# A softmax with relative-position bias: loads and stores on two queues, rows in one long run per partition

## The chip, the cores and the metric

The kernel runs on one core of a Trainium2 chip. The metric is the device time of one execution in microseconds; the time before is the median of three runs, 1329.67 us (1329.32 to 1330.35). One more execution was taken with the hardware profiler. Times inside it are counted from its first instruction.

The engines that matter here are VectorE (DVE in the profile), ScalarE (ACT), GpSimd (POOL), SyncE (SP), which issues transfers, and the 16 DMA engines, which move data between the memory (HBM) and the on-chip buffer. Each of SyncE and ScalarE has a queue of its own into the DMA engines; a transfer is cut into packets, one contiguous run of bytes each.

## What is computed

```python
B, H, S, max_rel = 2, 8, 2112, 16
rel = pos[:, None] - pos[None, :]                       # row minus column
bias = rel_bias[:, np.clip(rel, -16, 16) + 16]          # (H, S, S) from (H, 33)
x = logits + bias[None]                                 # logits: (B, H, S, S) float32
x = x - x.max(axis=-1, keepdims=True)
out = exp(x) / exp(x).sum(axis=-1, keepdims=True)
```

There are 2 x 8 x 2112 = 33,792 rows of 2112 floats, 8448 bytes each, so 285.5 MB are read and as much is written. The bias of a row is a constant on the far left, a constant on the far right and a ramp of 33 values around the diagonal. Seen from one row to the next it only slides by one column, so a single strip that is longer than a row holds the bias of all neighbouring rows as windows of it.

## The kernel before

**Tiling.** A partition owns blocks of W = 33 consecutive rows. 64 partitions hold one head and the other 64 the next head, so one pass of the outer loop (k, of K = 4) covers two heads of both batches. Within a pass, a block is cut into chunks of 6, 5, 6, 5, 6 and 5 rows for each batch, NT = 12 chunks, 48 in all. A chunk is one buffer of four (`X0` to `X3`): 128 partitions with 5 or 6 rows each, loaded by one transfer and stored by one transfer, one packet of 41 or 50 KB for each partition.

**The strip.** At the start of each pass `strip(k)` builds, on DVE, the strip `F` of the two heads (lines 143 to 158). The table `rel_bias` comes in once, by a small transfer on ScalarE's queue (line 107).

**One chunk.** `add(m)` waits for the chunk's load and then runs, for each row, one DVE instruction (line 173) that adds the strip's window, negates and keeps the row's extreme. `exps(m)` runs the exponential of each row on ACT (line 181), each as soon as its add is done, and sums it. `scale(m)` waits on DVE for all exponentials of the chunk, takes the reciprocals (line 189) and scales the first DV = 3 rows (line 193); `scale_rest(m)` scales the other 2 or 3 on ACT (line 198). Only then does DVE start the next chunk's adds.

**Queues.** All large transfers are issued by SyncE in one order that is written out by hand, `turn`: store chunk n, wait until the store of chunk n - 1 has landed, load chunk n + 3 into the buffer that it has freed. Before a store, SyncE waits for the scaled rows (semaphores `scaled` and `scaledA`). Loads and stores thus stand in one queue, one behind the other. The last chunk is stored in two parts, 3 and 2 rows. DVE, ACT and SyncE run loops (`Fori`) over the passes; inside a pass everything is written out.

Of the kernel before, what the change touches and what calls it, by code (L numbers as in the profile page):

```python
# [15 lines left out]
def kernel(  # L16
# [6 lines left out]
    nc = tc.nc  # L23
# [2 lines left out]
    assert S == S2  # L26
    MR = 16
    W = 2 * MR + 1
    NB = S // W
    K = H // 2  # L30
    assert NB * W == S and 2 * NB == P and H % 2 == 0
    FW = S + W - 1
    BIG = 3.0e38
    NBUF = 4
    SIZES = [6, 5, 6, 5, 6, 5]
    R = max(SIZES)
    assert sum(SIZES) == W

    CH = [(b, sum(SIZES[:i]), r) for b in range(B) for i, r in enumerate(SIZES)]
    NT = len(CH)  # L40
    assert NT % NBUF == 0
# [3 lines left out]
    F = io.tile([P, FW], FP32, tag="F", name="F")  # L45
    rbP = io.tile([P, H // 2, W], FP32, tag="rbP", name="rbP")
    rbK = io.tile([P, W], FP32, tag="rbK", name="rbK")
    rest = io.tile([P, NB], FP32, tag="rest", name="rest")
    nmax = io.tile([P, NBUF * R], FP32, tag="nmax", name="nmax")
    tot = io.tile([P, NBUF * R], FP32, tag="tot", name="tot")  # L50
    rec = io.tile([P, NBUF * R], FP32, tag="rec", name="rec")
    ps = ctx.enter_context(tc.tile_pool(name="ps", bufs=1, space=bass.MemoryType.PSUM))
    Z = ps.tile([P, 512], FP32, tag="Z", name="Z")
    eq, lt, gt = (Z[:, i * NB : (i + 1) * NB] for i in range(3))
# [12 lines left out]

    with tc.tile_critical(no_gpsimd_drain=True):  # L68
# [13 lines left out]
        def take(eng, sem, n):  # L82
            eng.wait_ge(sem, n).then_inc(sem, -n)  # L83


        def load(k, m):
            b, r = m % NBUF, CH[m][2]
            nc.sync.dma_start(out=X[b][:, 0 : r * S], in_=rows(logits, k, m, 0, r)).then_inc(ld[b], 16)

        def store(k, m, s0=0, n=None):  # L90
            b, n = m % NBUF, n or CH[m][2]
            if s0 < DV:
                take(nc.sync, scaled, DV)
            if s0 + n > DV:
                take(nc.sync, scaledA, s0 + n - DV)
            nc.sync.dma_start(
                out=rows(out, k, m, s0, n), in_=X[b][:, s0 * S : (s0 + n) * S]
            ).then_inc(st[b], 16)

        for m in range(NBUF):  # L100
            load(0, m)

        Q = 32
        step = list(F.ap[0])[0]
        nc.vector.memset(F[:, 0 : H * W], 0.0).then_inc(zero, 1)  # L105
        nc.scalar.wait_ge(zero, 1)
        nc.scalar.dma_start(
            out=bass.AP(tensor=F.tensor, offset=F.offset, ap=[[Q * step, P // Q], [1, H * W]]),
            in_=bass.AP(tensor=rel_bias.tensor, offset=rel_bias.offset, ap=[[0, P // Q], [1, H * W]]),
        ).then_inc(rb, 16)  # L110
        for p0 in (0, NB):
            nc.gpsimd.iota(  # L112
                F[p0 : p0 + NB, H * W : H * W + NB], pattern=[[-1, NB]], base=0,
                channel_multiplier=1, allow_small_or_imprecise_dtypes=True,
            ).then_inc(idx, 1)

        v = nc.vector
        done = [0]
# [11 lines left out]
        iq = F[:, H * W : H * W + NB]  # L130
        for m, op in ((eq, ALU.is_equal), (lt, ALU.is_gt), (gt, ALU.is_lt)):
            then(v.tensor_scalar(out=m, in0=iq, scalar1=0.0, scalar2=None, op0=op))  # L132
        v.wait_ge(rb, 16)
        then(v.stream_shuffle(out=F[:, 0 : H * W], in_=F[:, 0 : H * W], mask=[0] * Q))  # L134
        settle()
        for h in range(2):
            p = slice(h * NB, (h + 1) * NB)
            src = bass.AP(tensor=F.tensor, offset=F[p].offset + h * W,
                          ap=[[list(F.ap[0])[0], NB], [2 * W, K], [1, W]])
            then(v.tensor_copy(out=rbP[p], in_=src))  # L140
        settle()

        def strip(k):

            then(v.tensor_copy(out=rbK[:, :], in_=rbP[:, bass.ds(k, 1), :]))  # L145
            settle()
            low, high = rbK[:, W - 1 : W], rbK[:, 0:1]
            blocks = view(F, MR, [[W, NB], [1, W]])
            then(v.tensor_tensor(out=blocks, in0=view(eq, 0, [[1, NB], [0, W]]),  # L149
                                 in1=view(rbK, W - 1, [[0, NB], [-1, W]]), op=ALU.mult))  # L150
            then(v.tensor_scalar(out=rest, in0=lt, scalar1=low, scalar2=None, op0=ALU.mult))  # L151
            then(v.tensor_copy(out=F[:, 0:MR], in_=low.to_broadcast([P, MR])))  # L152
            then(v.tensor_copy(out=F[:, FW - MR : FW], in_=high.to_broadcast([P, MR])))  # L153
            settle()
            then(v.scalar_tensor_tensor(out=rest, in0=gt, scalar=high, in1=rest, op0=ALU.mult, op1=ALU.add))  # L155
            settle()
            then(v.tensor_tensor(out=blocks, in0=blocks, in1=view(rest, 0, [[1, NB], [0, W]]), op=ALU.add))  # L157
            settle()

        def row(m, i):  # L160
            return X[m % NBUF][:, i * S : (i + 1) * S]
# [2 lines left out]
            c = m % NBUF * R + i  # L164
            return t[:, c : c + n]

        DV = 3

        def add(m):
            take(v, ld[m % NBUF], 16)  # L170
            j, r = CH[m][1:]
            for i in range(r):
                v.tensor_tensor_reduce(  # L173
                    out=row(m, i), in0=row(m, i), in1=F[:, W - 1 - j - i : W - 1 - j - i + S],
                    scale=-1.0, scalar=BIG, op0=ALU.add, op1=ALU.min, accum_out=col(nmax, m, i),
                ).then_inc(added, 1)

        def exps(m):
            for i in range(CH[m][2]):
                take(nc.scalar, added, 1)  # L180
                nc.scalar.activation(  # L181
                    out=row(m, i), in_=row(m, i), func=ACTF.Exp, scale=-1.0, bias=col(nmax, m, i),
                    accum_out=col(tot, m, i),
                ).then_inc(expd, 1)

        def scale(m):
            r = CH[m][2]
            take(v, expd, r)
            v.reciprocal(out=col(rec, m, 0, r), in_=col(tot, m, 0, r)).then_inc(inv, 1)  # L189
            v.wait_ge(inv, 1).then_inc(inv, -1)  # L190
            v.sem_inc(invA, 1)
            for i in range(DV):
                v.tensor_scalar_mul(out=row(m, i), in0=row(m, i), scalar1=col(rec, m, i)).then_inc(scaled, 1)  # L193

        def scale_rest(m):
            take(nc.scalar, invA, 1)
            for i in range(DV, CH[m][2]):
                nc.scalar.activation(  # L198
                    out=row(m, i), in_=row(m, i), func=ACTF.Copy, scale=col(rec, m, i),
                ).then_inc(scaledA, 1)  # L200
# [19 lines left out]
        store(0, 0)  # L220
        with nc.Fori(0, K - 1, 1, engines=[ENG.SP]) as k:
            turn(k, 1, NT + 1)
        turn(K - 1, 1, NT - 3)
        for m in range(NT - 3, NT - 1):
            store(K - 1, m)
        r = CH[NT - 1][2]
        store(K - 1, NT - 1, 0, DV)
        store(K - 1, NT - 1, DV, r - DV)
        for b in range(NBUF):
            take(nc.sync, st[b], 32 if b == (NT - 1) % NBUF else 16)  # L230


# [28 lines left out]
```

## Time and profile before

| | before |
|---|---|
| median of the runs | 1329.67 us |
| the profiled execution's own time | 1329.3 us |
| its span, first to last instruction | 1327.5 us |
| DVE busy | 819.7 us, 62% |
| ACT busy | 808.8 us, 61% |
| SyncE's DMA queue: packets' time as a share of 16 engines | 99.8% |
| moved | 571.00 MB, mean 430 GB/s |

In the lines of the profile an instruction stands with its line in the kernel, its engine, its operation and its operands (`out<-in`, partitions x elements). In the windows each line has the stretch in microseconds, its length, the busy time of DVE, ACT and POOL with the number of instructions, a clock (of an engine that isn't used here), the share of time in which the 16 DMA engines were busy, and the GB/s that they moved. A packet is counted where it is recorded, so short windows scatter around 1.00 and a share can read 1.03. In the timeline a line has its start, its length and the instruction; where several follow each other on one line, the length is that of all together with the pauses between. "DVEq", "ACTq" and "SPq" are the engines' instruction queues. A row of the groups has the total busy time and the mean of one instruction in ns.

### The profile page before, as it was taken

Reading aid. Unit: us, or ns where it says so; the run is one execution under the profiler, and the core shown is the slowest. Engines: PE = TensorE matmul, PEld = TensorE weight load, DVE = VectorE, ACT = ScalarE, POOL = GpSimd, SP = SyncE. Lnnn points to the kernel's source line nnn. Section 1 sums busy time; section 2 is a strip of 40 time slices with the busy share of each in tenths; the row PEclk is TensorE's granted clock in tenths of the full one; section 3 lists DMA queues with packets and bytes.
Section 4 is the critical chain, followed back from the end, with each engine's and each line's share of the span. In section 5 each row is a group of like instructions: output and inputs, shape, how many; then the busy total and the mean of one; then the engine's idle time right before and its main releaser. Section 6 shows DMA issues by size and latency. Waiting matters only on the chain. (4 is left out here: it accounts for less than half of the span.)

```text
span 1327.5 us, 2383 instructions
## 1 busy us (share of the span) xinstructions
DVE 819.7 (62%) x756; ACT 808.8 (61%) x652; POOL 0.6 (0%) x6
## 2 busy tenths in 40 slices
DVE  6875665558655566556866466664686547665572
ACT  3885575655756557555676566764667646675472
POOL 0000000000000000000000000000000000000000
DMA  9999999999999999999999999999999999999998
GB/s 407 427 424 425 430 433 429 432 431 433 434 430 438 423 439 431 432 432 433 438 436 429 433 430 435 433 430 441 427 439 428 435 431 437 434 436 427 436 427 376
DMA packets 13981, 571.00 MB, mean 430 GB/s; under 512 B 1556, under 2 KB 1560, under 8 KB 1560
## 3 DMA queue, kind: packets, MB, share of 16 engines
q1 hardware_dynamic: 13968, 570.96, 99.8%
q14 instruction: 5, 0.04, 0.0%
q10 hardware_dynamic: 8, 0.00, 0.0%
HBM read 285.48 MB, written 285.47 MB: 430 GB/s over the span
## 5 line engine op out<-in xcount | busy, mean ns | idle before, releaser
L173 DVE CUSTOM_DVE_ANT_0 X<-X,F 128x2112 f32<-128x2112 f32 x264 | 605.5, 2354 | 346.8 <-DVEq L83 346.8
L181 ACT ACTIVATE X<-X,nmax 128x2112 f32<-128x2112 f32 x264 | 542.2, 2054 | 411.5 <-ACTq L83 385.7
L198 ACT ACTIVATE X<-X,rec 128x2112 f32<-128x2112 f32 x120 | 238.7, 2046 | 29.0 <-ACTq L83 29.0
L193 DVE TENSOR_SCALAR X<-X,rec 128x2112 f32<-128x2112 f32 x144 | 181.4, 1316 | 11.6 <-DVEq L190 11.6
L189 DVE RECIPROCAL rec<-tot 128x6 f32<-128x6 f32 (+1 forms) x48 | 9.1, 190 | 116.1 <-DVEq L83 116.1
L181 ACT ACTIVATION_READ_ACCUMULATOR X<-X,nmax 128x1 f32 x264 | 49.3, 187 | 0.0
L181 ACT ACT_TABLE_LOAD x4 | 5.1, 1283 | 55.8 <-ACTq L83 55.8
L173 DVE DVE_READ_ACCUMULATOR2_ANT nmax<- 128x1 f32 x264 | 21.7, 82 | 0.0
L157 DVE TENSOR_TENSOR F<-F,rest 128x2112 f32<-128x2112 f32 x4 | 9.4, 2358 | 0.6
L149 DVE TENSOR_TENSOR F<-Z,rbK 128x2112 f32<-128x2112 f32 x4 | 9.4, 2358 | 0.6
L134 DVE LOAD_MASK_SELECT F<-F x1 | 0.0, 14 | 7.1 <-DMA F<-in_rel_bias_dram 7.1
L155 DVE SCALAR_TENSOR_TENSOR rest<-Z,rbK,rest 128x64 f32<-128x64 f32 x4 | 1.1, 284 | 0.6 <-DVEq L83 0.2
L151 DVE TENSOR_SCALAR rest<-Z,rbK 128x64 f32<-128x64 f32 x4 | 1.1, 275 | 0.0
L105 DVE MEMSET F<- 128x264 f32 x1 | 0.3, 278 | 1.1 <-SPq L68 1.1
L145 DVE COPY rbK<-rbP 128x33 f32 x4 | 0.7, 178 | 0.3 <-DVEq L83 0.3
L153 DVE COPY F<-rbK 128x16 f32<-128x16 f32 x4 | 0.7, 168 | 0.0
L152 DVE COPY F<-rbK 128x16 f32<-128x16 f32 x4 | 0.7, 166 | 0.0
L132 DVE TENSOR_SCALAR Z<-F 128x64 f32<-128x64 f32 x3 | 0.5, 223 | 0.1
L140 DVE COPY rbP<-F 64x132 f32<-64x132 f32 x2 | 0.4, 224 | 0.2
L134 DVE STREAM_SHUFFLE F<-F 128x264 f32<-128x264 f32 x1 | 0.4, 443 | 0.0
L112 POOL IOTA F<- 64x64 f32 x2 | 0.4, 179 | 0.7 <-PEq L256 0.6
L245 POOL MEMSET const-bfloat16-1.0<- 128x1 bf16 x1 | 0.1, 103 | 0.0
(3 smaller groups left out, 0.3 us busy)
## 6 DMA issues: line engine op xcount, KB each, us to landing
X<-in_logits_dram SPq DMA_DIRECT2D x24, 6336.0 KB, 39.7
out_dram<-X SPq DMA_DIRECT2D x24, 6336.0 KB, 46.9
X<-in_logits_dram SPq DMA_DIRECT2D x24, 5280.0 KB, 42.2
out_dram<-X SPq DMA_DIRECT2D x23, 5280.0 KB, 48.6
out_dram<-X SPq DMA_DIRECT2D x1, 3168.0 KB, 16.5
out_dram<-X SPq DMA_DIRECT2D x1, 2112.0 KB, 21.1
F<-in_rel_bias_dram ACTq DMA_DIRECT2D x1, 4.1 KB
```

The lines of the kernel that those rows point to most:

```text
L145: then(v.tensor_copy(out=rbK[:, :], in_=rbP[:, bass.ds(k, 1), :]))
L149: then(v.tensor_tensor(out=blocks, in0=view(eq, 0, [[1, NB], [0, W]]), in1=view(rbK, W - 1, [[0, NB], [-1, W]]), op=ALU.mult))
L151: then(v.tensor_scalar(out=rest, in0=lt, scalar1=low, scalar2=None, op0=ALU.mult))
L152: then(v.tensor_copy(out=F[:, 0:MR], in_=low.to_broadcast([P, MR])))
L153: then(v.tensor_copy(out=F[:, FW - MR : FW], in_=high.to_broadcast([P, MR])))
L155: then(v.scalar_tensor_tensor(out=rest, in0=gt, scalar=high, in1=rest, op0=ALU.mult, op1=ALU.add))
L157: then(v.tensor_tensor(out=blocks, in0=blocks, in1=view(rest, 0, [[1, NB], [0, W]]), op=ALU.add))
L173: v.tensor_tensor_reduce(out=row(m, i), in0=row(m, i), in1=F[:, W - 1 - j - i : W - 1 - j - i + S], scale=-1.0, scalar=BIG, op0=ALU.add, o ...
L181: nc.scalar.activation(out=row(m, i), in_=row(m, i), func=ACTF.Exp, scale=-1.0, bias=col(nmax, m, i), accum_out=col(tot, m, i),).then_inc( ...
L189: v.reciprocal(out=col(rec, m, 0, r), in_=col(tot, m, 0, r)).then_inc(inv, 1)
L193: v.tensor_scalar_mul(out=row(m, i), in0=row(m, i), scalar1=col(rec, m, i)).then_inc(scaled, 1)
L198: nc.scalar.activation(out=row(m, i), in_=row(m, i), func=ACTF.Copy, scale=col(rec, m, i),).then_inc(scaledA, 1)
```

## The change

A partition now owns RP = 264 consecutive rows of one head and one batch (eight partitions for a head and batch), so the rows of neighbouring partitions lie 264 rows apart in memory instead of 33. They are cut into 46 chunks of 2, 4, 42 times 6, 4 and 2 rows. One strip of S + RP - 1 columns, different for each partition, serves the whole run; it is built once, with masks made from the partition number. The loops are gone: every instruction is written out. SyncE issues the loads alone, the load of chunk m after the store of chunk m - 4 has landed. ScalarE issues the stores, each after it has scaled its own rows and waited for DVE's. Of a chunk of r rows DVE scales r // 2 and ACT the rest. There are still four buffers of six rows.

```diff
+    RP = B * H * S // P
+    NB = S // RP
+    FW = S + RP - 1
-    SIZES = [6, 5, 6, 5, 6, 5]
-    CH = [(b, sum(SIZES[:i]), r) for b in range(B) for i, r in enumerate(SIZES)]
+    R = 6
+    SIZES = [2, 4] + [6] * 42 + [4, 2]
+    NT = len(SIZES)
+    FIRST = [sum(SIZES[:m]) for m in range(NT)]
...
-    def rows(t, k, m, s0, n):
-        b, j, r = CH[m]
+    def rows(t, m):
         return bass.AP(
-            tensor=t.tensor,
-            offset=t.offset + (b * H * S + j + s0) * S + k * (2 * S * S),
-            ap=[[W * S, P], [1, n * S]],
+            tensor=t.tensor, offset=t.offset + FIRST[m] * S, ap=[[RP * S, P], [1, SIZES[m] * S]],
         )
...
+        def dv(m):
+            return SIZES[m] // 2
+
+        def store(m):
+            b = m % NBUF
+            take(nc.scalar, scaled, dv(m))
+            take(nc.scalar, scaledA, SIZES[m] - dv(m))
+            nc.scalar.dma_start(out=rows(out, m), in_=X[b][:, 0 : SIZES[m] * S]).then_inc(st[b], 16)
+
+        for m in range(NT):
+            if m >= NBUF:
+                take(nc.sync, st[m % NBUF], 16)
+            load(m)
+        for m in range(NT - NBUF, NT):
+            take(nc.sync, st[m % NBUF], 16)
...
+        then(v.stream_shuffle(out=T, in_=T, mask=[0] * Q))
+        then(v.tensor_tensor(out=heads, in0=view(F, 0, [[W, H], [1, W]]), in1=view(hsel, 0, [[1, H], [0, W]]),
+                             op=ALU.mult))
+        then(v.tensor_reduce(out=rbK, in_=view(F, H * W, [[1, W], [W, H]]), axis=mybir.AxisListType.X, op=ALU.add))
...
+        then(v.tensor_tensor(out=bands, in0=bands, in1=view(rest, 0, [[1, NB], [0, W]]), op=ALU.add))
+        then(v.tensor_copy(out=view(F, C0 + W, [[RP, NB - 1], [1, RP - W]]),
+                           in_=view(reg, 1, [[1, NB - 1], [0, RP - W]])))
+        then(v.tensor_copy(out=F[:, 0:C0], in_=reg[:, 0:1].to_broadcast([P, C0])))
+        then(v.tensor_copy(out=F[:, last:FW], in_=reg[:, NB : NB + 1].to_broadcast([P, FW - last])))
...
         def add(m):
             take(v, ld[m % NBUF], 16)
-            j, r = CH[m][1:]
-            for i in range(r):
+            for i in range(SIZES[m]):
+                x = RP - 1 - FIRST[m] - i
                 v.tensor_tensor_reduce(
-                    out=row(m, i), in0=row(m, i), in1=F[:, W - 1 - j - i : W - 1 - j - i + S],
+                    out=row(m, i), in0=row(m, i), in1=F[:, x : x + S],
...
-        with nc.Fori(0, K, 1, engines=[ENG.DVE]) as k:
-            strip(k)
-            for m in range(NT):
-                add(m)
-                scale(m)
-        with nc.Fori(0, K, 1, engines=[ENG.Activation]):
-            for m in range(NT):
-                exps(m)
-                scale_rest(m)
-        def turn(k, first, stop):
-            for n in range(first, stop):
-                store(k + n // NT, n % NT)
-                take(nc.sync, st[(n - 1) % NBUF], 16)
-                load(k + (n + 3) // NT, (n + 3) % NT)
...
+        for m in range(NT):
+            add(m)
+            scale(m)
+        for m in range(NT):
+            exps(m)
+            scale_rest(m)
+            store(m)
```

More of the change, by code (lines that the diff above doesn't have):

```diff
@@ L28 @@
     W = 2 * MR + 1
[L29 to L32, printed above, removed]
+    RP = B * H * S // P
+    NB = S // RP
+    assert NB * RP == S and RP * P == B * H * S and P // NB == B * H
+    FW = S + RP - 1
     BIG = 3.0e38
     NBUF = 4
-    SIZES = [6, 5, 6, 5, 6, 5]
-    R = max(SIZES)
-    assert sum(SIZES) == W
-    CH = [(b, sum(SIZES[:i]), r) for b in range(B) for i, r in enumerate(SIZES)]
-    NT = len(CH)
-    assert NT % NBUF == 0
+    R = 6
+    SIZES = [2, 4] + [6] * 42 + [4, 2]
+    assert sum(SIZES) == RP
+    NT = len(SIZES)
+    FIRST = [sum(SIZES[:m]) for m in range(NT)]
     io = ctx.enter_context(tc.tile_pool(name="io", bufs=1))
     X = [io.tile([P, R * S], FP32, tag=f"X{b}", name=f"X{b}") for b in range(NBUF)]
[L45 to L48, printed above, removed]
+    F = io.tile([P, FW + 1], FP32, tag="F", name="F")
+    pid = io.tile([P, 2], I32, tag="pid", name="pid")
+    own = io.tile([P, W + 2 * NB + 1], FP32, tag="own", name="own")
+    rbK, rest, reg = own[:, 0:W], own[:, W : W + NB], own[:, W + NB : W + 2 * NB + 1]
     nmax = io.tile([P, NBUF * R], FP32, tag="nmax", name="nmax")
@@ L51, with small @@
     rec = io.tile([P, NBUF * R], FP32, tag="rec", name="rec")
+    num = rec[:, 0 : NB + 1]
     ps = ctx.enter_context(tc.tile_pool(name="ps", bufs=1, space=bass.MemoryType.PSUM))
     Z = ps.tile([P, 512], FP32, tag="Z", name="Z")
-    eq, lt, gt = (Z[:, i * NB : (i + 1) * NB] for i in range(3))
+    zc = [0]
+    def small(n):
+        zc[0] += 16 * -(-n // 16)
+        return Z[:, zc[0] - 16 * -(-n // 16) : zc[0] - 16 * -(-n // 16) + n]
+    eq, lt, hsel = (small(NB) for _ in range(3))
+    le, gt = (small(NB + 1) for _ in range(2))
+    qh = small(2)
     def view(t, offset, dims):
         return bass.AP(tensor=t.tensor, offset=t.offset + offset, ap=[[list(t.ap[0])[0], P]] + dims)
-    def rows(t, k, m, s0, n):
-        b, j, r = CH[m]
+    def rows(t, m):
         return bass.AP(
-            tensor=t.tensor,
-            offset=t.offset + (b * H * S + j + s0) * S + k * (2 * S * S),
-            ap=[[W * S, P], [1, n * S]],
+            tensor=t.tensor, offset=t.offset + FIRST[m] * S, ap=[[RP * S, P], [1, SIZES[m] * S]],
         )
@@ L83, in take, with load @@
             eng.wait_ge(sem, n).then_inc(sem, -n)
[L86 to L115, printed above, removed]
+        def load(m):
+            b = m % NBUF
+            nc.sync.dma_start(out=X[b][:, 0 : SIZES[m] * S], in_=rows(logits, m)).then_inc(ld[b], 16)
+        def dv(m):
+            return SIZES[m] // 2
+        def store(m):
+            b = m % NBUF
+            take(nc.scalar, scaled, dv(m))
[7 more added lines that the diff above has]
+            take(nc.sync, st[m % NBUF], 16)
         v = nc.vector
@@ L126, in settle @@
             done[0] = 0
-        v.wait_ge(idx, 2)
-        iq = F[:, H * W : H * W + NB]
-        for m, op in ((eq, ALU.is_equal), (lt, ALU.is_gt), (gt, ALU.is_lt)):
-            then(v.tensor_scalar(out=m, in0=iq, scalar1=0.0, scalar2=None, op0=op))
+        Q = 32
+        step = list(F.ap[0])[0]
+        T = F[:, 0 : H * W]
+        v.memset(T, 0.0).then_inc(zero, 1)
+        nc.scalar.wait_ge(zero, 1)
+        nc.scalar.dma_start(
+            out=bass.AP(tensor=F.tensor, offset=F.offset, ap=[[Q * step, P // Q], [1, H * W]]),
+            in_=bass.AP(tensor=rel_bias.tensor, offset=rel_bias.offset, ap=[[0, P // Q], [1, H * W]]),
+        ).then_inc(rb, 16)
@@ new lines @@
+        nc.gpsimd.iota(pid[:, :], pattern=[[0, 2]], base=0, channel_multiplier=1).then_inc(idx, 1)
+        nc.gpsimd.iota(
+            num, pattern=[[1, NB + 1]], base=0, channel_multiplier=0,
+            allow_small_or_imprecise_dtypes=True,
+        ).then_inc(idx, 1)
+        v.wait_ge(idx, 2)
+        then(v.tensor_scalar(out=pid[:, 0:1], in0=pid[:, 0:1], scalar1=NB - 1, scalar2=None, op0=ALU.bitwise_and))
+        then(v.tensor_scalar(out=pid[:, 1:2], in0=pid[:, 1:2], scalar1=3, scalar2=H - 1,
+                             op0=ALU.logical_shift_right, op1=ALU.bitwise_and))
@@ L133 @@
+        settle()
+        then(v.tensor_copy(out=qh, in_=pid[:, :]))
+        settle()
+        q, h = qh[:, 0:1], qh[:, 1:2]
+        for o, n, s, op in ((eq, NB, q, ALU.is_equal), (lt, NB, q, ALU.is_lt), (hsel, NB, h, ALU.is_equal),
+                            (le, NB + 1, q, ALU.is_le), (gt, NB + 1, q, ALU.is_gt)):
+            then(v.tensor_scalar(out=o, in0=num[:, 0:n], scalar1=s, scalar2=None, op0=op))
         v.wait_ge(rb, 16)
-        then(v.stream_shuffle(out=F[:, 0 : H * W], in_=F[:, 0 : H * W], mask=[0] * Q))
+        then(v.stream_shuffle(out=T, in_=T, mask=[0] * Q))
@@ L135 @@
         settle()
[L136 to L140, printed above, removed]
-        settle()
[L143 to L158, printed above, removed]
@@ new lines @@
+        heads = view(F, H * W, [[W, H], [1, W]])
+        then(v.tensor_tensor(out=heads, in0=view(F, 0, [[W, H], [1, W]]), in1=view(hsel, 0, [[1, H], [0, W]]),
+                             op=ALU.mult))
+        settle()
+        then(v.tensor_reduce(out=rbK, in_=view(F, H * W, [[1, W], [W, H]]), axis=mybir.AxisListType.X, op=ALU.add))
+        settle()
+        low, high = rbK[:, W - 1 : W], rbK[:, 0:1]
+        C0 = RP - 1 - MR
+        bands = view(F, C0, [[RP, NB], [1, W]])
+        then(v.tensor_scalar(out=rest, in0=lt, scalar1=low, scalar2=None, op0=ALU.mult))
@@ new lines @@
+        then(v.tensor_scalar(out=reg, in0=le, scalar1=low, scalar2=None, op0=ALU.mult))
+        settle()
+        then(v.scalar_tensor_tensor(out=rest, in0=gt[:, 0:NB], scalar=high, in1=rest, op0=ALU.mult, op1=ALU.add))
+        then(v.scalar_tensor_tensor(out=reg, in0=gt, scalar=high, in1=reg, op0=ALU.mult, op1=ALU.add))
+        then(v.tensor_tensor(out=bands, in0=view(eq, 0, [[1, NB], [0, W]]), in1=view(rbK, W - 1, [[0, NB], [-1, W]]),
+                             op=ALU.mult))
+        settle()
@@ L178, in exps @@
         def exps(m):
-            for i in range(CH[m][2]):
+            for i in range(SIZES[m]):
                 take(nc.scalar, added, 1)
@@ L191, in scale @@
             v.sem_inc(invA, 1)
-            for i in range(DV):
+            for i in range(dv(m)):
                 v.tensor_scalar_mul(out=row(m, i), in0=row(m, i), scalar1=col(rec, m, i)).then_inc(scaled, 1)
@@ L196, in scale_rest @@
             take(nc.scalar, invA, 1)
-            for i in range(DV, CH[m][2]):
+            for i in range(dv(m), SIZES[m]):
                 nc.scalar.activation(
```

16 lines of the change are left out of this document (3 added, 13 removed).

## The prediction

> **What bounds the kernel now.** I read the page first, its engine shares and its DMA lines, then the windows by stage, the DMA issues, the waits and the timeline of the first chunk and of the end.
>
> ```profile
> span 1327.5 us, 2383 instructions
> DVE 819.7 (62%) x756; ACT 808.8 (61%) x652; POOL 0.6 (0%) x6
> DMA  9999999999999999999999999999999999999998
> DMA packets 13981, 571.00 MB, mean 430 GB/s; under 512 B 1556, under 2 KB 1560, under 8 KB 1560
> q1 hardware_dynamic: 13968, 570.96, 99.8%
> q14 instruction: 5, 0.04, 0.0%
> ```
>
> Neither compute engine is busy two thirds of the span, while the 16 DMA engines are busy in all 40 slices: one queue, SyncE's, moves 570.96 MB and its packets take 99.8% of what the engines have. The kernel is bound by bytes, and the bytes are fixed: every logit is read once and every result written once. What can change is the rate, and the stretches where the rate is not reached. The windows show both (length, DVE, ACT and POOL busy, clock, DMA share, GB/s):
>
> ```profile
> 0.00:20.00 20.00, 8.59 (x16) 0.00 (x0) 0.56 (x6) 1.00 0.95 392
> 20.00:40.00 20.00, 17.26 (x17) 18.30 (x16) 0.00 (x0) 1.00 1.03 446
> 40.00:60.00 20.00, 17.34 (x17) 16.52 (x14) 0.00 (x0) 1.00 0.95 392
> 60.00:100.00 40.00, 30.10 (x28) 33.08 (x27) 0.00 (x0) 1.00 1.03 438
> 100.00:200.00 100.00, 62.40 (x56) 61.52 (x51) 0.00 (x0) 1.00 0.99 427
> 200.00:300.00 100.00, 56.52 (x51) 58.04 (x46) 0.00 (x0) 1.00 1.00 432
> 300.00:600.00 300.00, 185.17 (x171) 183.36 (x148) 0.00 (x0) 1.00 1.00 433
> 600.00:900.00 300.00, 189.10 (x173) 187.45 (x151) 0.00 (x0) 1.00 1.00 433
> 900.00:1200.00 300.00, 186.82 (x171) 183.35 (x148) 0.00 (x0) 1.00 1.00 434
> 1200.00:1305.00 105.00, 66.37 (x60) 67.14 (x54) 0.00 (x0) 1.00 1.00 431
> 1305.00:1320.00 15.00, 0.00 (x0) 0.02 (x1) 0.00 (x0) 1.00 0.96 416
> 1320.00:1327.50 7.50, 0.00 (x0) 0.00 (x0) 0.00 (x0) 1.00 0.47 199
> ```
>
> The best long stretch runs at 434 GB/s with a share of 1.00; I take that as the rate of the engines when nothing disturbs them. 571.0 MB / 434 GB/s = 1315.7 us. The other 11.8 us are what the windows lose against 434, each as length x (434 - rate) / 434: start (0 to 40 us) 1.9 - 0.6 = 1.4; the time in which loads and stores first alternate (40 to 300 us) 1.9 - 0.4 + 1.6 + 0.5 = 3.6; the long middle (300 to 1305 us) 0.7 + 0.7 + 0 + 0.7 = 2.1; the end 0.6 + 4.1 = 4.7. The reader is to see that only these 11.8 us, 0.9% of the time, can be won at all.
>
> **Is the compute covered?** The timeline of the first chunk of six rows (start, length) and SyncE's issues:
>
> ```profile
> 0.97 1.88 SPq L88 DMA_DIRECT2D X<-in_logits_dram  x4
> 1.39 1.10 ACTq L107 DMA_DIRECT2D F<-in_rel_bias_dram  x1
> 9.08 0.44 DVE L134 STREAM_SHUFFLE F<-F 128x264 f32<-128x264 f32 x1
> 18.60 2.36 DVE L173 CUSTOM_DVE_ANT_0 X<-X,F 128x2112 f32<-128x2112 f32 x1 [2.15 <-DVEq L83]
> 20.89 2.35 DVE L173 CUSTOM_DVE_ANT_0 X<-X,F 128x2112 f32<-128x2112 f32 x1
> 32.28 0.08 DVE L173 DVE_READ_ACCUMULATOR2_ANT nmax<- 128x1 f32 x1
> 35.30 3.78 DVE L193 TENSOR_SCALAR X<-X,rec 128x2112 f32<-128x2112 f32 x3 [0.24 <-DVEq L190]
> 35.33 5.95 ACT L198 ACTIVATE X<-X,rec 128x2112 f32<-128x2112 f32 x3 [0.61 <-ACTq L83]
> 38.99 2.35 DVE L173 CUSTOM_DVE_ANT_0 X<-X,F 128x2112 f32<-128x2112 f32 x1
> 1226.88 0.33 SPq L96 DMA_DIRECT2D out_dram<-X  x1
> 1286.66 2.36 DVE L173 CUSTOM_DVE_ANT_0 X<-X,F 128x2112 f32<-128x2112 f32 x1 [7.08 <-DVEq L83]
> ```
>
> The adds of two chunks start 38.99 - 18.60 = 20.4 us apart. The same six rows need a load and a store of 6336 KB (6.49 MB, 14.95 us at 434 GB/s each), so 29.9 us of the DMA engines. Compute has 9.5 us to spare in every chunk.
>
> **The change, part by part.**
>
> Bytes: the same rows in and out, so 1315.7 us at the undisturbed rate. There are 46 loads and 46 stores where there were 48 and 49; of these, five completions fewer. No row prices a completion by itself; between nothing and the 434-to-431 difference of the quieter windows it is under a microsecond in all, and I take nothing.
>
> DVE: three of four bias strips go. The rows of one strip are
>
> ```profile
> L149 DVE TENSOR_TENSOR F<-Z,rbK 128x2112 f32<-128x2112 f32 x4 | 9.4, 2358 | 0.6
> L157 DVE TENSOR_TENSOR F<-F,rest 128x2112 f32<-128x2112 f32 x4 | 9.4, 2358 | 0.6
> L198 ACT ACTIVATE X<-X,rec 128x2112 f32<-128x2112 f32 x120 | 238.7, 2046 | 29.0 <-ACTq L83 29.0
> L193 DVE TENSOR_SCALAR X<-X,rec 128x2112 f32<-128x2112 f32 x144 | 181.4, 1316 | 11.6 <-DVEq L190 11.6
> ```
>
> so about 2 x 2.36 us and some small ones each, 15 us off DVE in all. Half of every chunk is scaled on DVE: 1 + 2 + 42 x 3 + 2 + 1 = 132 rows instead of 144, and ACT takes 132 instead of 120. DVE loses 12 x 1.32 = 16 us, ACT gains 12 x 2.05 = 25 us. All of it lies under the DMA engines: worth nothing.
>
> ACT's queue: each store now waits on ACT for DVE's and ACT's scaled rows and is issued there, ahead of the next chunk's exponentials, for which DVE's scaling of that chunk waits in turn. DVE's three rows end at 39.08 and ACT's at 41.28, so the wait is for ACT's own rows, and what is new is the issue. ACT's only issue so far took 1.10 us, SyncE's stores 0.33 us; I take the larger. The chunk's period rises from 20.4 to about 21.5 us against 29.9: 8.4 us of cover are left, cost nothing. SyncE keeps only the loads, each behind the landing of the store four chunks earlier.
>
> Both rings full? A load is issued when a store has landed. If loads and stores share the engines half and half, each 6-row transfer lasts 29.9 us; of a buffer's round of 4 x 29.9 = 120 us, transfers take 60 and compute 21.5, which leaves 38 us of queueing in one ring or the other. So there is always something to move, as now.
>
> The start: the first four loads hold 2 + 4 + 6 + 6 = 18 rows (before, 22), 19.5 MB or 45 us, so the engines have work until 47 us. The first store must be issued before that. The table lands at 9.08 as now. The new strip follows: shuffle 0.44, two operations over 264 elements at about the same, four of up to 9 elements at 0.3 or less, two over 264 elements, and fills of 7 x 231, 247 and 248 elements, at 2.36 us per 2112 about 2.4 us; with the gaps some 7.5 us, done at about 17 us. Two rows of add (2.28 each, 20.89 after 18.60), then 3.0 us until scaling (35.30 after 32.28), a table load of about a microsecond, 2 us of scaling: the first store goes out at about 28 us. 19 us of cover; the start costs what it costs now, 1.4 us.
>
> The end: now the last load is in at 1286.66, and what follows is 16 rows of stores, 17.3 MB, 39.9 us at 434: 1326.5. The engines are never empty, and the 4.7 us lost are unequal finishes of the 16 engines. With the change, when the store of the last-but-four chunk lands, four chunks (6, 6, 4, 2 rows) are still to store, 19.5 MB or 45 us, and the last load (2 rows, 5 us) is on its way. In the shared engines it lands within 20 us; the chunks of 4 and 2 rows need some 16 and 10 us of compute by the rows above, so the last store is issued about 41 us on, and the rings are empty only after 50. The cover is 9 us; beyond it each microsecond would count in full. I take the same 4.7 us.
>
> The unrolled code: no loop means that all instructions are fetched once instead of a quarter of them four times. Before, five fetches fell in the span; three of them here:
>
> ```profile
> q14 instruction: 3, 0.02, 0.1%
> ```
>
> (this is the DMA answer for 210 to 260 us). The window from 200 to 300 us, which holds them, lost 0.5 us, so at most 0.15 us for each. Some 15 more make 0 to 2.3 us; I take nothing, since the other windows lose as much without fetches.
>
> **The alternation.** This is the term that decides. Now an engine changes from loads to stores about every 13.7 us (1327.5 us / 97 transfers). With two rings it can change at every packet: 12,400 large packets / 16 engines make 8 per transfer, so up to 46 x 2 x 8 = 736 changes for each engine instead of about 95. What does a change cost? From below: 900 to 1200 us holds some 22 changes and loses nothing. Between: 300 to 900 us holds 44 and loses 1.4 us, 0.03 us each. From above: 40 to 300 us holds 19 and loses 3.6 us, 0.19 us each. The price falls as the run goes on, though each transfer is the same, so I read it as a cost of all 16 engines turning together, which ends when they have drifted apart. Interleaved rings should drift apart as quickly, so I take the same 3.6 us for the first time and 2.1 us for the rest: the sum is 1315.7 + 1.4 + 3.6 + 2.1 + 4.7 = 1327.5 us. The profiled execution took 1329.3 us for its span of 1327.5, 1.8 us around it; the median of the runs, 1329.67, is 0.4 us above that. The forecast is 1329.3 us: no change that can be measured (0.2%, 2.7 us, is about what a measurement of this kernel tells from none).
>
> **The rivals.**
>
> Faster: with loads and stores mixed at all times there is no moment at which all engines turn from one to the other, and the 3.6 and 2.1 us vanish; the smaller last packets (2 rows) may level the finishes. For it: the losses do fall to nothing once the engines are apart. Against it: two lock-stepped rings start in step as well. 1327.5 - 5.7 = 1321.8, or 1323.6 us as a time; with 1.5 us off the end, 1322. Chance 0.31.
>
> Slower, by the change at each packet: if the 0.03 us of the middle windows belongs to each change, 736 - 95 = 641 more cost 19 us: 1348 us. At 0.19 us it would be 122 us, 1451 us. It decides from 4 ns for each change (2.7 us / 641). For it: the losses of the first 300 us do stand where loads and stores first meet. Against it: 434 GB/s over 300 us with changes in it. Chance 0.22.
>
> Slower, by the stride: a partition's rows lie 264 rows apart in memory instead of 33, 2,230,272 bytes instead of 278,784, and the 16 engines walk rows that far apart in step. If that meets a bottleneck in the memory, the rate falls in all windows. No row shows such a stride; the lowest full-queue window, 392 GB/s, would give 571.0 / 392 = 1457 us and as little as 2% 1356 us; a better spread than now would show nothing, since the share is 1.00 already. Chance 0.08. The Trainium skill, DMA: Bandwidth & Descriptors, in Latency and other measured facts, gives 164 GB/s per direction for a row pitch of 2 MiB and full speed, 214, when a large pitch is padded by 4 KiB. The new pitch is 2 MiB and 130 KiB, so by that rule it counts as padded; were it not, the estimate from the page's two rates would be 1315.7 x 214 / 164 = 1717 us. No trace here shows it yet.
>
> Slower, by the end or the fetches: if the last chunk's compute is 10 us later than I count, or the fetches cost their upper bound on the one engine that finishes last, 3 to 6 us: 1332 to 1335 us. Chance 0.06.
>
> **How the numbers follow.** No change 0.33 (1327 to 1332), faster 0.31, slower 0.22 + 0.08 + 0.06 = 0.36. The time is that of the likeliest case, 1329.3. Its own range is 1327 to 1332; since both signs hold much of the chance, the range goes down to the faster rival with its levelled end, 1322, and up to the middle price of the change, 1348. Left out are the stride and the dearer changes, about 0.15.
>
> **What would show it.** Right: the loads' and stores' queues share the bytes half and half, the windows from 300 us on show 433 to 434 GB/s at a share of 1.00, DVE and ACT still wait on DMA in every full chunk, and the first store leaves near 28 us. The faster rival shows in 434 GB/s from about 60 us on; the dearer changes in a share near 1.00 with 425 to 431 GB/s throughout; the stride in a low rate in the loads alone, before the first store. The forecast is wrong if the share drops under 1.00 in the middle: then the rings do run empty, and the queueing sum above is wrong.

## The result and the profile after

The changed kernel takes 1338.18 us against 1329.65 before: a ratio of 1.0062, with a 95% interval of 1.0050 to 1.0075. It is slower by 8.5 us; the forecast was no change, 1329.3. Its profiled execution took 1338.4 us for a span of 1336.6.

The page of the changed kernel, its first lines and its DMA queues:

```profile
span 1336.6 us, 2180 instructions
DVE 786.6 (59%) x728; ACT 829.7 (62%) x661; POOL 0.4 (0%) x6
DMA  9999999999999999999999999999999999999995
q1 hardware_dynamic: 6624, 285.48, 49.6%
q10 hardware_dynamic: 6632, 285.48, 49.4%
q14 instruction: 17, 0.14, 0.0%
```

The two queues share the bytes half and half, the compute engines are no busier than they were, and one line has tripled: 17 instruction fetches instead of 5. The windows of the changed kernel, in coarser stretches than before's:

```profile
0.00:40.00 40.00, 26.91 (x42) 20.81 (x17) 0.43 (x6) 1.00 0.98 406
40.00:300.00 260.00, 156.94 (x143) 168.62 (x135) 0.00 (x0) 1.00 1.00 433
300.00:1305.00 1005.00, 594.07 (x537) 629.91 (x503) 0.00 (x0) 1.00 1.00 433
1305.00:1320.00 15.00, 7.21 (x7) 8.19 (x6) 0.00 (x0) 1.00 0.72 311
1320.00:1336.60 16.60, 1.49 (x2) 2.17 (x3) 0.00 (x0) 1.00 0.37 157
```

Reckoned against 434 GB/s as in the prediction, the start loses 2.6 us (1.4 before), 40 to 300 us 0.6 (3.6 before), the middle 2.3 (2.1 before by the finer windows), and the end 4.3 + 10.6 = 14.9 (4.7 before). So the end costs 10.2 us more than before, and the rest of the run wins 1.6. In these last 32 us the DMA engines stand idle for nearly half of the time, though the work isn't done. The issues of that stretch, and the last chunk's first add:

```profile
1251.86 28.25 SPq L90 DMA_DIRECT2D X<-in_logits_dram  x2
1259.73 0.34 ACTq L99 DMA_DIRECT2D out_dram<-X  x1
1290.03 0.34 ACTq L99 DMA_DIRECT2D out_dram<-X  x1
1309.41 0.34 ACTq L99 DMA_DIRECT2D out_dram<-X  x1
1313.18 2.36 DVE L184 CUSTOM_DVE_ANT_0 X<-X,F 128x2112 f32<-128x2112 f32 x1 [5.38 <-DVEq L86]
1322.87 0.34 ACTq L99 DMA_DIRECT2D out_dram<-X  x1
```

The last load, two rows of 2.2 MB in all, is issued at the end of the first line, 1280 us, and its chunk starts only at 1313.18. It takes 33 us for what the engines move in 5 at 434 GB/s.

Who is late is seen in the trace one level down. Each transfer is done by all 16 DMA engines, and each of them reports its own share: in the trace the semaphore of every large transfer is raised 16 times. For the last transfers of the changed kernel (L loads, S stores, by chunk), the moment when the middle one of the 16 reports and when the last one does, in us:

```
         L44     L45     S41     S42     S43     S44     S45
middle   1279.4  1290.0  1263.8  1285.6  1306.3  1320.7  1329.2
last     1293.0  1313.0  1279.7  1303.0  1320.5  1330.4  1335.5
```

One engine is 14 us and more behind the middle one in the work that it has done. A transfer is done when the last engine has done its share: load 45 waited for store 41 until 1279.7, while most engines had finished that store at 1263.8. They then ran out of work, and the late engine went on, one transfer after the other, to 1335.5. How far the latest three engines are behind the middle one, for transfers between 1100 and 1260 us, in the profiled execution of each run, with its fetches in the span and the run's time (the engines are told apart here by who is last, not by number; for two queues the loads' and stores' lags stand apart, since a late engine's queues need not be late alike):

```
                                     fetches  loads              stores             us
before                                 5      2.0  1.5  1.4      as loads           1329.65
the changed kernel                    17     11.9  9.3  3.0      15.7 13.0  6.7     1338.18
before, loops written out             18      7.0  5.5  1.4      as loads           1334.14
before, code added on GpSimd          22     11.8  5.6  4.3      as loads           1336.60
before, two queues                     5      6.0  4.9  4.3      16.5  4.9  4.4     1339.07
changed, one queue                    17     11.1 10.5  7.5      as loads           1334.70
changed, ScalarE and SyncE looped      9     11.8  5.3  2.5      13.3  6.6  3.9     1336.01
changed, all chunks of six rows       18      5.1  1.8  1.4      20.8 10.2  6.0     1337.09
five rows, two queues                 17      4.9  3.4  1.5      11.3  9.6  6.2     1331.56
five rows, two queues, loops           4      3.5  0.4  0.3       3.5  2.4  0.4     1329.16
five rows, one queue                  17      9.1  7.8  7.0      as loads           1333.75
five rows, one queue, loops            4      6.6  6.6  5.7      as loads           1331.49
five rows, two queues, smaller end     4      2.8  0.4  0.3       2.8  2.4  0.4     1327.05
```

The packets show what a fetch does. It is a packet of 8192 bytes that takes 309 ns on one engine, and the next data packet of that engine is late as well. In the changed kernel the packets right behind the 17 fetches took 116 to 629 ns more than usual (1872 ns for 50,688 bytes), 371 on average: 0.68 us for each fetch, 11.6 us for all, on the few engines that serve them. Other slow packets between 110 and 1280 us make 20 us more. Together that is about what the three late engines are behind, 30 us. By following each engine's packets end to start, most of these others fall to the engines that serve fetches, but that assignment is approximate. Slow packets alone are no loss: in the kernel before they make some 40 us in the same stretch, more than in the change, but followed in this way they fall on all 16 engines, 0.9 to 5.1 us each, so none is far behind.

### The profile page after: what moved, and what is told of

Same layout as the page of the kernel before. It is cut to its first block, busy times and chain, and to the rows that moved or that the text cites. A ratio compares the mean times of both kernels' runs of the same rounds, so it can differ in the third digit from the quotient of the medians.

```text
span 1336.6 us, 2180 instructions
## 1 busy us (share of the span) xinstructions
DVE 786.6 (59%) x728; ACT 829.7 (62%) x661; POOL 0.4 (0%) x6
## 5 line engine op out<-in xcount | busy, mean ns | idle before, releaser
L209 ACT ACTIVATE X<-X,rec 128x2112 f32<-128x2112 f32 x132 | 261.9, 2045 | 28.5 <-ACTq L86 28.5
L204 DVE TENSOR_SCALAR X<-X,rec 128x2112 f32<-128x2112 f32 x132 | 166.5, 1316 | 11.5 <-DVEq L201 11.5
L200 DVE RECIPROCAL rec<-tot 128x6 f32<-128x6 f32 (+2 forms) x46 | 8.7, 190 | 112.7 <-DVEq L86 112.7
```

Of the source, the lines that this page charges most:

```text
L209: nc.scalar.activation(out=row(m, i), in_=row(m, i), func=ACTF.Copy, scale=col(rec, m, i),).then_inc(scaledA, 1)
```

## The experiments

The theory that the lags suggest: **instruction fetches of the written-out code make the engines that serve them late, and the last engine sets the end.** The rivals: the turns of two queues cost the time, the long stride does, or the order at the end.

**Two queues in the kernel before.** Loops, strips and 33-row blocks stay; the last chunk, stored in parts of 3 and 2 rows before, now goes in one transfer.

```diff
+            take(nc.scalar, scaled, DV)
+            take(nc.scalar, scaledA, n - DV)
+            nc.scalar.dma_start(out=rows(out, k, m, 0, n), in_=X[b][:, 0 : n * S]).then_inc(st[b], 16)
...
                 scale_rest(m)
...
+                store(k, m)
```

> The kernel before with its stores issued by ScalarE and SyncE left with the loads, loops, blocks of 33 rows and strips as before. Theory of the fetches (instruction fetches of the written-out code throw the DMA engine that serves them out of step, and that engine, late by 10 us and more, sets the end): few fetches here, so the slowest engine is not late, the windows show 433 to 434 GB/s to the end, 1322 to 1327 us. Theory of the two rings (packets of two queues by turns cost the slowest engine its time): as slow as the change, 1336 to 1339 us.

Measured: 1339.07 us, 1.0068 (1.0045 to 1.0092). A miss for the theory of the fetches, which gave 1322 to 1327; taken alone, this run fits the two rings, which gave 1336 to 1339. There are five fetches here, as before. The windows and two moments of its end:

```profile
900.00:1200.00 300.00, 187.39 (x174) 185.72 (x152) 0.00 (x0) 1.00 1.00 431
1305.00:1320.00 15.00, 11.12 (x12) 12.89 (x12) 0.00 (x0) 1.00 0.56 243
```

```profile
1300.67 2.36 DVE L169 CUSTOM_DVE_ANT_0 X<-X,F 128x2112 f32<-128x2112 f32 x1 [6.09 <-DVEq L83]
1319.25 0.34 ACTq L94 DMA_DIRECT2D out_dram<-X  x1
```

The last chunk's adds start at 1300.67, where the kernel before started them at 1286.66 with 16 rows of stores still queued. Here the stores have taken turns with the loads, so they are nearly done when the last load comes; 18.6 us of compute and five rows of store then stand alone. By these rows two queues have a cost at the end that has nothing to do with fetches; no run parts it from the late engine. For one engine was also 16.5 us behind in the stores (6.0 in the loads), some 8 of it before 220 us; why, stays open.

**The loops of the kernel before written out**, `for k in range(K)` in place of the three `Fori`, nothing else.

> The kernel before with its loops written out, everything else unchanged, one queue. Theory of the fetches: about 17 fetches in the span instead of 5, slowest engine later, 1332 to 1338 us. Theory of the two rings: one ring, so as before, 1329 to 1330.5 us.

Measured: 1334.14 us, 1.0035 (1.0023 to 1.0048), 18 fetches. Within the fetches' range, outside the other. One queue, the short stride and the old chunks are all there, so 4.6 us are the price of the written-out code alone. Its fetches and its end:

```profile
q14 instruction: 18, 0.15, 0.0%
...
1305.00:1320.00 15.00, 3.21 (x3) 3.46 (x2) 0.00 (x0) 1.00 0.95 407
1320.00:1331.70 11.70, 0.00 (x0) 0.00 (x0) 0.00 (x0) 1.00 0.26 110
```

**The changed kernel with one queue**: stores issued by SyncE in the order of before.

> The changed kernel with its stores on SyncE's queue in the order of before (store n, wait for store n - 1, load n + 3), still written out, 264 rows to a partition. Theory of the fetches alone: still slow, 1334 to 1338 us. Theory of the two rings: 1328 to 1331 us. If both are needed (a fetch throws an engine out of step, and only with two rings does it keep falling behind): between, 1330 to 1334 us. The stride, if it cost anything, would show here as a rate under 433 GB/s in the middle.

Measured: 1334.70 us, 1.0043 (1.0027 to 1.0060): in the range of the fetches, at its lower edge. Its middle:

```profile
300.00:1305.00 1005.00, 594.36 (x538) 631.29 (x504) 0.00 (x0) 1.00 1.00 433
```

The long stride costs nothing, and 5 us stay, about as many as the written-out code cost before. One queue takes off 3.5 us by the medians, 2.5 by the two ratios; the intervals of the ratios overlap (1.0050 to 1.0075 for the change), so this part is likely rather than shown.

**ScalarE's and SyncE's middle chunks in loops**, DVE still written out.

```diff
+        with nc.Fori(0, 10, 1, engines=[ENG.Activation]) as t:
+            for j in range(NBUF):
+                exps(2 + j)
+                scale_rest(2 + j)
+                store(2 + j, t)
...
```

> The changed kernel with ScalarE's and SyncE's 40 middle chunks in loops of four, DVE still written out. Theory of the fetches: about half of the 17 fetches go, one of the two late engines with them; the one that serves DVE's fetches stays late, 1330 to 1337 us, and no more than one engine is over 5 us late. Theory of the two rings: 1338 us, as many engines late as before.

Measured: 1336.01 us, 1.0042 (1.0028 to 1.0056), 9 fetches. One of the two late engines drops from about 11 us behind to 6; the other stays, and with it most of the time. Both are still over 5 us behind, where the theory allowed one. The intervals of this run and the change overlap a little, so the lags speak more clearly here than the time.

**More code beside the kernel before.** The clean dose: one queue, loops, and instructions on the idle GpSimd that touch no data. DVE raises the semaphore `pace` once for each chunk.

```diff
+        for m in range(K * NT):
+            take(nc.gpsimd, pace, 1)
+            for i in range(22):
+                nc.gpsimd.sem_inc(fill, 1)
+                take(nc.gpsimd, fill, 1)
```

> The kernel before, one queue and loops, and beside it some 2000 instructions on the idle GpSimd that only count a semaphore up and down, 45 for each chunk, so that its code is fetched through the whole run; no data is touched by them. Theory of the fetches (what counts is the load on the DMA engine that serves them): 16 more fetches on one DMA engine, that engine ends 4 to 8 us later, 1333 to 1337 us. If instead the written-out code costs because DVE or ScalarE wait for their own instructions: nothing, 1329 to 1330.5 us.

Measured: 1336.60 us, 1.0053 (1.0036 to 1.0070). The engines and queues on its page, and the windows of its end:

```profile
DVE 819.6 (61%) x756; ACT 808.8 (61%) x652; POOL 0.6 (0%) x6
...
q1 hardware_dynamic: 13968, 570.96, 99.1%
q14 instruction: 22, 0.18, 0.0%
```

```profile
1305.00:1320.00 15.00, 5.59 (x6) 7.75 (x6) 0.00 (x0) 1.00 0.72 310
1320.00:1336.00 16.00, 0.00 (x0) 0.00 (x0) 0.00 (x0) 1.00 0.44 189
```

Neither DVE nor ScalarE nor a large transfer has changed, and 0.14 MB more of instructions cost 7 us. In the lags one engine runs from 3.0 us behind at 200 us to 11.8; it ends at 1334.8, 7.5 us behind the middle one. Followed end to start, its packets hold all but three of the 18 fetches between 100 and 1280 us, and these 15, at 0.31 us each and 0.29 for the packet behind, make 9 us of the 9.8 by which the lag exceeds that of the kernel before (11.8 against 2.0). So it is the load on one DMA engine, not DVE or ScalarE waiting for their code, and little is left for the counting of the semaphores itself. This settles that fetches by themselves cost such a kernel microseconds; how much of the change's 8.5 they make is for the other runs.

**Without the small chunks at the ends**, 44 times six rows.

> The changed kernel with 44 chunks of six rows, without the small ones at the start and the end. If the end is set by the late DMA engine's own work, which is the same: 1337 to 1340 us. If it is set by emptied rings (the last load comes late because the stores take turns with it, and then a chunk's compute and store stand alone): 20 us of compute and 15 us of store instead of 10 and 5 stand at the end, 1346 to 1358 us.

Measured: 1337.09 us, 1.0080 (1.0053 to 1.0107), 18 fetches. The median is the change's: with an engine 20 us late in the stores it mostly makes no difference whether the last chunk has six rows or two, the late engine's own work sets the end. But three of the nine executions took 1342, 1345 and 1351 us, the last as the theory of the emptied rings had it; the profile is of a short one, so what made them long isn't known.

**Five rows to a chunk, written out and with loops.** With smaller buffers there is room for a copy of the strip's window at a fixed place, which the loop on DVE needs.

```diff
-    SIZES = [2, 4] + [6] * 42 + [4, 2]
+    SIZES = [2, 3] + [5] * 51 + [2, 2]
...
+        with nc.Fori(0, 12, 1, engines=[ENG.DVE]) as t:
+            window(t)
+            for j in range(NBUF):
+                add(2 + j, t)
+                scale(2 + j)
...
```

> The changed kernel with chunks of five rows (2, 3, 51 times 5, 2, 2), still written out, two queues. It is the pair of the next run, since only with smaller buffers is there room for that one. Both theories: about as the change, 1336 to 1342 us, two DMA engines 8 us and more behind the others.

> The run before with 48 of the 51 middle chunks in loops of four on DVE, ScalarE and SyncE (DVE copies the loop turn's window of the strip to a fixed place, which it can afford). Two queues, long stride and small last chunks stay. Theory of the fetches: few fetches in the span, no engine more than 5 us behind, 1323 to 1329 us. Theory that two rings alone make engines fall behind: 1335 us and more, as without loops.

Measured: 1331.56 us, 1.0016 (1.0006 to 1.0025) written out, and 1329.16 us, 0.9996 (0.9987 to 1.0006) with loops. The first is a miss: five rows alone took 6.6 us off the change, with as many fetches. With loops 4 fetches are left and no engine is over 3.5 us behind, as the theory had it; the time lies just above its range. What it still loses is the end:

```profile
40.00:300.00 260.00, 157.14 (x144) 181.68 (x142) 0.00 (x0) 1.00 1.01 435
300.00:1305.00 1005.00, 581.92 (x533) 672.52 (x525) 0.00 (x0) 1.00 1.00 433
1305.00:1320.00 15.00, 6.13 (x6) 6.35 (x5) 0.00 (x0) 1.00 0.72 309
1320.00:1327.90 7.90, 0.00 (x0) 0.00 (x0) 0.00 (x0) 1.00 0.58 246
```

**The last four stores behind the last load**, issued by SyncE: tried on the kernel before with two queues, on the change, and on five rows with loops.

```diff
+        for m in range(NT - NBUF, NT):
+            store(m, eng=nc.sync)
```

> The kernel before with two queues (the first experiment), except that the stores of the last four chunks are issued by SyncE behind the last load, so that no store takes turns with the last loads. If the cost of two queues in that kernel sits in its end (the last load comes late, the stores that should cover its compute are done): 1339 falls to 1325 to 1330 us, and the DMA share from 1305 us on is near 1. If it sits in the turns of the two rings through the run: 1336 to 1340 us as before.

> The changed kernel with the stores of its last four chunks issued by SyncE behind the last load. If the late DMA engine's own work sets the end (it is busy until the last store whatever the order): 1336 to 1339 us. If the order at the end costs too: about 3 us less than the change, 1334 to 1335 us.

> Chunks of five rows with loops and two queues, and the stores of the last four chunks issued by SyncE behind the last load. Here no engine is far behind, and what is left is the end (share 0.72 from 1305 to 1320 us). If the order of the end causes it: 1323 to 1327 us, faster than before; if not: 1328.5 to 1330 us as without.

Measured: 1342.17 us, 1.0091 (1.0070 to 1.0112); 1337.04 us, 1.0064 (1.0047 to 1.0081); 1329.96 us, 1.0001 (0.9992 to 1.0010). The first is above both of its ranges, the other two are in the range for no gain. In the first, ScalarE's last pass is written out too, with 8 fetches instead of 5. The edit opens a new hole: SyncE waits for a store to land on the slowest engine before it issues the last load, and the stores that would fill the wait stand behind it. The last of the three shows the old hole closed and the new one open:

```profile
1260.00:1290.00 30.00, 18.38 (x17) 21.11 (x18) 0.00 (x0) 1.00 0.87 350
1290.00:1305.00 15.00, 9.18 (x10) 12.27 (x11) 0.00 (x0) 1.00 1.02 434
1305.00:1320.00 15.00, 1.49 (x2) 2.21 (x3) 0.00 (x0) 1.00 0.98 422
```

So these runs don't tell how much the end costs where it stands. The change stays at 1337 with this order, as the late engine's own work would demand; but its four executions lie between 1334.8 and 1339.9, and in the profiled one, the shortest, the last engine is only 9.5 us behind.

**Two by two.** The same five-row kernels with one queue:

> Chunks of five rows, written out, all transfers in SyncE's queue in the order of before. Pair of the two-queue run with the same sizes (1331.6 us). If two queues cost by themselves: 1326 to 1329 us. If they cost only in the end of the run or by engines that are late already: 1330 to 1333 us, one engine 8 us and more behind the others.

> The run before with the middle 48 chunks in loops. Pair of the two-queue loop run (1329.2 us). Theory of the fetches: 2 to 5 us less than written out, no engine over 5 us behind, 1325 to 1329 us. If the queues cost by themselves, it is clearly under 1329.2; if not, 1328 to 1330 us.

Measured: 1333.75 us, 1.0029 (1.0019 to 1.0040), and 1331.49 us, 1.0014 (1.0005 to 1.0023). Both are above all that was expected of them. In the second three engines are 5.7 to 6.6 us behind, where no more than 5 were expected, although none of its 4 fetches falls between 71 and 1299 us: an engine can be late without fetches.

| five rows | written out | loops |
|---|---|---|
| one queue | 1333.75 | 1331.49 |
| two queues | 1331.56 | 1329.16 |

The written-out code costs 2.3 to 2.4 us with either queueing. The second queue gains 2.2 to 2.3 us by the medians. The pairs for that were taken on different chips, each with the kernel before beside it; by the ratios it is 1.7 and 2.4 us, and the intervals overlap a little. With six rows the second queue lost 2.5 to 3.5.

**A smaller end.** Last chunks of 3 and 1 rows, and the odd row of a chunk scaled on DVE.

> The two-queue loop kernel with last chunks of 3 and 1 rows instead of 2 and 2, and the odd row of a chunk scaled on DVE. If what is left is the last chunk's compute (9.7 us) and store (5 us), standing alone: both halve, 1324 to 1327 us, faster than before. If the end is set by the DMA engines' own work: 1328.5 to 1330 us.

Measured: 1327.05 us, 0.9980 (0.9971 to 0.9989): faster than the kernel before by 2.7 us, the only one that is. Its end:

```profile
1305.00:1320.00 15.00, 3.85 (x4) 2.15 (x2) 0.00 (x0) 1.00 0.96 413
1320.00:1325.50 5.50, 0.00 (x0) 0.00 (x0) 0.00 (x0) 1.00 0.14 58
```

The hole from 1305 us is filled (0.96 where it was 0.72), as it should be if the last chunk's compute and store set the end when no engine is late. The share of the odd row isn't parted from it: it moves work from ScalarE to DVE in every chunk.

## Why the prediction was wrong, step by step

**Bound by bytes, 434 GB/s as the undisturbed rate:** right. From 300 to 1200 us the windows of the changed kernel show 433 to 434 GB/s, and with one queue 432 to 434. Only the kernel before with two queues falls below, to 430 and 431.

**Bytes, DVE's and ScalarE's share, the store's issue on ScalarE:** right in their effect. The issue took 0.34 us, not the 1.10 that was taken; DVE's first row starts at 12.49 us and the first store leaves at 23.21, earlier than the 28 that were reckoned. None of it was on the path.

**The stride:** that it costs nothing is right, at 433 GB/s in 300 to 1305 us. The Trainium skill, DMA: Bandwidth & Descriptors, Latency and other measured facts, holds that a large row pitch padded by a few KiB runs at full speed; this trace agrees, with 2 MiB and 130 KiB at 433 GB/s for loads and stores together.

**The alternation:** the price of a change of direction at each packet was bounded between nothing and 0.19 us; the windows say nothing at all. 40 to 300 us lost 0.6 us where 3.6 were taken over from before. That part of the faster rival came true, its 2.1 us of the middle did not (2.3). But its reason isn't shown: the kernel before with two queues loses the same 3.6 us there (428 GB/s), and the changed kernel with one queue 1.8 (431).

**The unrolled code: this step failed.** "At most 0.15 us for each. Some 15 more make 0 to 2.3 us; I take nothing." The bound divided a window's loss by three fetches as if 16 engines shared it. A fetch falls on one engine, 0.3 us for itself and 0.4 on average for the packet behind it, and, as the run with code on GpSimd shows, the fetches of one instruction queue fall on the same engine. In the changed kernel, where every engine is busy all the time, the last engine doesn't catch up: in the loads it is 3.8 us behind from 200 to 400 us, 6.8 from 400 to 600 and 11.1 from 800 to 1000, and the end belongs to it. A loss that the windows show spread over 16 engines can be 16 times that on the one that has it. Written-out code alone cost 4.6 us in the kernel before, and code that does nothing 7. So some 5 of the change's 8.5 us, what stays with one queue, are of the size that this step put at nothing; the other 2.5 to 3.5 go away with the second queue and are not explained. Nor are a loop's instructions fetched four times: the last of the five fetches before is at 250 us, in the first of the four passes. The Trainium skill, Runtime: NRT & Kernel Launch, Instruction fetch mechanics, calls the cost of a fetch mostly hidden and says that kernels prefer full unrolling, because of what a branch costs. No run here shows DVE or ScalarE waiting for code; but the DMA engines that bring it are not spared, and the loops were 2.3 to 4.6 us faster than the same code written out.

**The end: failed too, mostly as a consequence.** "I take the same 4.7 us" became 14.9. The last store was to be issued 41 us after the store of the last-but-four chunk had landed, and was issued 43 us after; that sum held. The cover was wrong: the rings were to be empty only after 50 us. The landing is that of the last engine, and the others had had that store 16 us earlier, so theirs were empty by then. The last load was to land within 20 us and took 33. On the late engine it began only at 1292.7, 13 us after its issue, and then its eight packets of 0.63 us started 2.5 us apart, in turns with 1.87 us packets of stores.

**The rivals:** the one by the end or the fetches, with 0.06 and 1332 to 1335 us, named the mechanism with half its size. Its upper bound was 3 to 6 us.

**Luck and signs:** that 1338.18 lies inside the stated range of 1322 to 1348 is luck, for its upper end came from the dear change of direction, which the windows refute. And most signs of being right came true (the bytes shared half and half, 433 to 434 GB/s at a share of 1.00 in the middle, DVE and ACT waiting on DMA) while the forecast was wrong: a mean over 16 engines can't show that one of them is late.

**Open:** why a late engine has slow packets of its own besides those behind fetches (20 us in the changed kernel, 4 to 5 in the five-row kernel with as many fetches), and why they fall evenly in the kernel before and on a few engines elsewhere; why two queues seem to lose with six rows and to gain with five; and why two queues in the kernel before left one engine 16 us behind in stores with five fetches. Of that last kernel's 9.5 us the end's share is argued from its rows, not shown by a run.

## What to carry to other kernels

Where the DMA engines are busy for the whole span, a loss on one engine can be a loss of the whole: look at when each engine of the 16 reports, not only at the mean share, and count everything that a single engine serves, instruction fetches first. Written-out code is not free there; loops on long bodies were worth 2 to 5 us here. And with loads and stores on two queues the last load takes turns with the stores that should cover its compute, so once no engine is late, the last chunks should be small.

## What was not expected

One fetch of 8 KB costs its engine 0.68 us, more than twice its own transfer of 0.31. Some 2000 instructions on an engine that takes no part made a kernel 0.5% slower. And in the changed kernel packets of two directions taking turns on all engines cost nothing in the middle: 433 to 434 GB/s from 100 to 1200 us.
